# A two-layer decoder trunk on one core: 24 recurrent weight blocks are split inside the first MLP's block stream, the inverse's matrices are sent ahead of the operand copies, and the last chunk's output copies are reordered

## The chip, the cores and the metric

One core of a Trainium2 chip runs the whole kernel in one launch. The metric is the device time of that core in microseconds (us), lower is better. TensorE is called PE in the profile, VectorE DVE, ScalarE ACT, GpSimd POOL and SyncE SP; the last three also issue DMAs.

## The reference

512 tokens of width 1024 go through two layers in float32; each layer adds a mixer and then an MLP to the residual x, and one RMS norm ends the trunk.

```python
h = rms_norm(x, mixer_norm[0]); x = x + dsa_mixer(h, ...)       # indexer, top-k keys, attention
x = x + sqrelu_mlp(rms_norm(x, mlp_norm[0]), up[0], down[0])    # 1024 -> 4096 -> 1024
h = rms_norm(x, mixer_norm[1]); x = x + rwkv7_mixer(h, ...)     # recurrent layer
x = x + sqrelu_mlp(rms_norm(x, mlp_norm[1]), up[1], down[1])
return rms_norm(x, final_norm)

def sqrelu_mlp(h, w_up, w_down):
    u = jax.nn.relu(h @ w_up)
    return (u * u) @ w_down

# inside rwkv7_mixer, per head, over the 512 steps:
sa = einsum('bhvk,bhk->bhv', state, -kk_t)
state = state * w_t + sa[..., None] * b_t + v_t[..., None] * k_t
y = einsum('bhvk,bhk->bhv', state, r_t)
```

## The kernel before

**Weights.** All weight matrices lie in device memory as blocks of 128 x 1024 floats (512 KB), in one list `wblk`. A product in float32 quality is made from three products of a cheaper type: each operand is cut into a high and a low part (hi, lo), and `gemm` (L143 to L150) sends hi x hi, hi x lo and lo x hi, 24 matmuls of 512 columns for a block. `c.order` is the order in which blocks are used. `wdma` issues the next load on SP's queue: a raw pair of 1 MB where two blocks follow each other in the list, a single one otherwise. `wload` makes the parts: an ACT copy to hi (L122) and a DVE subtraction to lo (L130 through `sub`). `wget` hands out the next split block, with `prefetch` running two or so ahead in program order. Raw and split blocks live in the same ring of 21 buffers (`b8`, 8 KB per partition) as x, the activations and the larger tiles of the recurrent layer.

**Blocks split ahead of their layer.** The recurrent layer uses 39 blocks (numbers relative to `BASE`): 0 to 7 for the keys, 8 to 10 for the low-rank decay and gate inputs, 11 and 12 for the output gate, 13 to 20 for r, 21 to 28 for v, 29 and 30 for the gate's second factor, 31 to 38 for the output product. For the 36 in `PRE`, `presplit` does the splitting during the first MLP: in half blocks, 72 steps, each a load on POOL's queue (L78, 256 KB), the ACT copy (L86), the DVE subtraction (L87) and two stores to a scratch tensor `scr` on POOL's queue (L91, 256 KB each). `mlp` advances it by `SD` = 2 steps at each of the 16 output blocks of both up products and of the 8 of the first down product, until the 72 are done. The recurrent layer then loads hi and lo from `scr` (L98, 1 MB) with no splitting. Block 0 is in a raw pair with the MLP's last block and is split where it is used.

**First MLP.** Two halves; each has 16 up blocks, an activation (`act`, L300 to L304: DVE, two ACT squares, DVE) and 8 down products of two blocks each. The last three columns of the second half are done in two token halves, and `Keys.first` runs beside them.

**Start of the recurrent layer.** `rwkv` makes the key product over k = 0 to 7 with eight banks open (L811 to L813). For each k, `prep2` makes the mixed input and its parts (L757, L764, L766, L133, L130), and `others` makes those for the other products, among them `xr`, the input of the r product. Then follow two r blocks (`rgemm`), the key norms, the low-rank products and the gate product (L949 to L951).

**Inverse.** The chunks of 64 tokens need the inverse of a triangular 64 x 64 matrix for each head and chunk. `invert` is a generator advanced by `run`. Its first two steps send the diagonal 32 x 32 blocks of `Mt` to a scratch `dn` (L1042, two sets of 8 DMAs on SP's queue; the second needs the last `Mt`); the third loads them back as `tn` (L1047); then come 30 pairs of DVE operations that depend on each other (L1054, L1056), advanced by a budget `RUNW` at each of the 8 blocks of the v product; then copies and DMAs back into `Mt`. `run` is called once in the loop over m (`RQ`), once after `acopy(0)` and `c.prefetch(3)`, then with `RUNW`. `acopy` (L1181) copies operands `AR` to another place, 8 DMAs on SP's queue a chunk.

**Order.** Up to the v product the framework orders each engine's instructions by program position, shifted by the numbers in `PR` (a positive one puts a site earlier), and by what it takes to be ready. Every engine then executes its list in order, and so does each queue. From `while not stage` on, the order is that of the program.

**Chunks.** For each of 8 chunks: `step_z` (a product, then two ACT copies L1304), `step_u` (a product L1310, then four ACT copies L1314), the state update, `step_r` and `step_y`. `opn(n + 1, 1)` makes the second half of the next chunk's operands, with DVE masks (L1208). `out(0)` makes the first 256 tokens' input of the output product: eight steps of a DVE operation (L1413), an ACT copy to hi (L133) and a subtraction to lo on DVE or POOL. After the last chunk, `wom(0, m)` uses all eight.

Of the kernel before, what the change touches and what calls it, by code (L numbers as in the profile page):

```python
# [19 lines left out]
class Ctx:  # L20
# [51 lines left out]
    def presplit(s):  # L72
        nc = s.nc
        jobs = [(j, slice(h * 512, h * 512 + 512)) for j in s.scr for h in range(2)]

        def load(j, cs):
            raw = s.t("praw")
            nc.gpsimd.dma_start(raw, s.aps["wblk"][j][:, cs])  # L78
            return raw

        raws = [load(*v) for v in jobs[:2]]
        for i, (j, cs) in enumerate(jobs):
            r = raws.pop(0)
            hi, lo = s.t("phi", F32R), s.t("plo", F32R)
# [205 lines left out]
def mlp(c, x, mi, done, mid, side=iter(())):  # L290
# [15 lines left out]
    for half in range(2):  # L306
        s = Act(c, "s", 16)
        for m in range(16):
            for _ in range(SD):
                next(side, None)  # L310
            p = c.bank("g")
            c.gemm(p, c.wget(), a)
            wait.append((p, *s(m)))
            if rstd is None:
                if m == 0:
                    mi.n.stat()
                    continue
                rstd = mi.n.spread()
            while wait:
                act(*wait.pop(0))  # L320
        for m in range(KC - HM if half else KC):
            for _ in range(0 if half else SD):
                next(side, None)
# [475 lines left out]
def rwkv(c, x, ks, gi):  # L799
# [382 lines left out]

    acopy(0)
    c.prefetch(3)
    run(1)

    def opnd(n):
        if n > 1:
# [511 lines left out]
```

## Time and profile before

| | us |
|---|---|
| median of 3 runs (lowest, highest) | 1376.36 (1374.78, 1379.29) |
| the profiled execution's own time | 1375.36 |
| its span in the trace | 1373.6 |
| busy in the span: PE, DVE, ACT, POOL | 1294.9, 779.2, 602.1, 282.9 |

Starts are counted from the span's start. A row's bracket tells how long the engine was idle before it and what released it. PEclk is the granted TensorE clock: 1.00 is 2.4 GHz, 0.5 is 1.2 GHz. The DMA share is the mean busy share of the core's 16 DMA engines. PE's busy time counts pipelined matmuls and says little alone; how many matmuls fall in a stretch says more.

### The profile page before, as it was taken

How to read it: one execution, taken by the hardware profiler on the slowest of the kernel's cores; microseconds unless marked ns; L12 is line 12 of the kernel's file. 1: busy time of each engine (PE TensorE's matmuls, PEld its weight loads, DVE VectorE, ACT ScalarE, POOL GpSimd, SP SyncE). 2: the span in 40 equal slices, each digit the busy share in tenths (PEclk: the TensorE clock that was granted, in tenths of full speed). 3: DMA queues.
4: the chain of work that ended last, by engine and by line, in shares of the span. 5: the costliest groups of instructions: out<-in, count | busy, mean ns of one | idle time of the engine just before them, and what ended most of it. 6: DMA issues, size and time to landing. Idle time of an engine off the chain costs nothing.

```text
span 1373.6 us, 20666 instructions
## 1 busy us (share of the span) xinstructions
PE 1294.9 (94%) x8197; PEld 1060.9 (77%) x8197; DVE 779.2 (57%) x1382; ACT 602.1 (44%) x1053; POOL 282.9 (21%) x388
## 2 busy tenths in 40 slices
PE   7989899989899989999999996977999999999997
PEld 6767566877688867889867885767998888888887
DVE  5689984546544455523968877365755532245422
ACT  5545693445532344411866423766244421134421
POOL 0386751055443143000000001164200000000000
PEclk9999999999999999999999998998999999999998
DMA  7100014388988786542442383235222222322401
GB/s 287 62 31 31 1 42 150 112 311 305 300 308 267 263 289 234 173 164 70 192 153 93 87 297 79 49 85 208 101 102 83 92 92 94 121 92 83 163 1 62
DMA packets 80592, 196.78 MB, mean 143 GB/s; under 512 B 36336, under 2 KB 39024, under 8 KB 75248
## 3 DMA queue, kind: packets, MB, share of 16 engines
q1 hardware_dynamic: 60976, 136.59, 29.1%
q0 software_dynamic: 17280, 56.64, 11.9%
q10 hardware_dynamic: 2240, 2.24, 0.5%
q8 instruction: 64, 1.05, 0.3%
q14 instruction: 32, 0.26, 0.1%
HBM read 148.77 MB, written 44.56 MB: 141 GB/s over the span
## 4 chain that ended last, share of the span: by engine, by line
PE 65%; DVE 11%; DMA 11%; ACT 5%; issue 4%; POOL 3%; SPq 0%; ACTq 0%; DVEq 0%; POOLq 0%
PE g L148 15%; PE g L150 15%; PE g L149 15%; DMA praw<-in_wblk 9%; PE g L661 2%; POOL scr L91 1%; ACT phi L86 1%; DVE pr L1054 1%; DVE tn L1056 1%; PE d L646 1%; DVE rot L444 1%; DVE w L130 1%; ACT w L122 1%; DVE L L620 1%; PE g L1310 1%
## 5 line engine op out<-in xcount | busy, mean ns | idle before, releaser
L130 DVE TENSOR_TENSOR w<-wraw,w 128x1024 fp32r<-128x1024 f32 x150 | 183.0, 1243 | 98.1 <-ACT w L122 98.1
L148 PE MATMUL g<-ah,w 128*128 128x512 f32 x512 | 203.8, 398 | 15.8 <-ACT w L122 15.8
L150 PE MATMUL g<-sh,w 128*128 128x512 f32 (+1 forms) x608 | 216.3, 356 | 0.4 <-DVE w L130 0.4
L148 PE MATMUL g<-sh,w 128*128 128x512 f32 (+1 forms) x608 | 216.5, 356 | 0.0
L149 PE MATMUL g<-sl,w 128*128 128x512 f32 (+1 forms) x608 | 216.2, 356 | 0.0
L150 PE MATMUL g<-ah,w 128*128 128x512 f32 x512 | 202.9, 396 | 0.6 <-DVE w L130 0.5
L149 PE MATMUL g<-al,w 128*128 128x512 f32 x512 | 202.5, 395 | 0.0
L122 ACT ACTIVATE w<-wraw 128x1024 fp32r<-128x1024 f32 x155 | 157.9, 1047 | 99.9 <-DMA wraw<-in_wblk 85.0
L150 PEld LDWEIGHTS g<-sh,w 128*128 128x128 f32 x608 | 114.9, 189 | 17.0 <-DVE w L130 0.8
L149 PEld LDWEIGHTS g<-sl,w 128*128 128x128 f32 x608 | 114.9, 189 | 16.3
L148 PEld LDWEIGHTS g<-sh,w 128*128 128x128 f32 x608 | 114.9, 189 | 16.2
L148 PEld LDWEIGHTS g<-ah,w 128*128 128x128 f32 x512 | 98.2, 192 | 37.6 <-ACT w L122 17.5
L150 PEld LDWEIGHTS g<-ah,w 128*128 128x128 f32 x512 | 98.0, 191 | 24.1 <-DVE w L130 3.6
L302 ACT ACTIVATE sh<-r 128x512 fp32r<-128x512 f32 x64 | 40.4, 631 | 168.8 <-DVE r L300 168.8
L149 PEld LDWEIGHTS g<-al,w 128*128 128x128 f32 x512 | 98.3, 192 | 20.3
L87 DVE TENSOR_TENSOR plo<-praw,phi 128x512 fp32r<-128x512 f32 x72 | 49.1, 689 | 71.8 <-ACT phi L86 68.9
L304 DVE TENSOR_TENSOR sl<-q,sh 128x512 fp32r<-128x512 f32 x64 | 44.3, 693 | 65.8 <-ACT q L303 65.2
L86 ACT ACTIVATE phi<-praw 128x512 fp32r<-128x512 f32 x72 | 44.8, 626 | 81.2 <-DMA praw<-in_wblk 73.3
L300 DVE SCALAR_TENSOR_TENSOR r<-g,rstd 128x512 f32<-128x512 f32 x64 | 43.9, 688 | 56.5 <-PE g L150 50.6
L91 POOL DMA_DIRECT2D scr<-phi x72 | 38.9, 541 | 177.0 <-ACT phi L86 176.5
L208 ACT ACTIVATE sq<-x 128x256 f32<-128x256 f32 (+1 forms) x56 | 26.7, 499 | 105.5 <-DVE x L328 57.2
L328 DVE TENSOR_TENSOR x<-g,x 128x512 f32<-128x512 f32 x26 | 17.8, 689 | 77.6 <-PE g L150 77.6
(321 smaller groups left out, 2570.1 us busy)
## 6 DMA issues: line engine op xcount, KB each, us to landing
wraw<-in_wblk SPq DMA_DIRECT2D x77, 1024.0 KB, 4.9
w<-scr SPq DMA_DIRECT2D x35, 1024.0 KB, 6.4
praw<-in_wblk POOLq DMA_DIRECT2D x72, 256.0 KB, 5.2
scr<-phi POOLq DMA_DIRECT2D x72, 256.0 KB, 5.1
scr<-plo POOLq DMA_DIRECT2D x72, 256.0 KB, 5.9
wraw<-in_wblk SPq DMA_DIRECT2D x4, 512.0 KB, 4.7
x<-in_xT SPq DMA_DIRECT2D x8, 256.0 KB, 5.2
x<-in_xT SPq DMA_DIRECT2D x2, 1024.0 KB, 6.6
```

The lines of the kernel that those rows point to most:

```text
L86: nc.scalar.activation(hi, r, AF.Copy)
L87: nc.vector.tensor_sub(lo, r, hi.bitcast(F32))
L91: nc.gpsimd.dma_start(s.scr[j][:, e, cs], v.bitcast(F32))
L122: s.wsp = s.nc.scalar.activation(hi, r, AF.Copy)
L130: s.nc.vector.tensor_sub(out, a, b)
L148: s.nc.tensor.matmul(p, whi[:, kc, :], ahi, start=first and kc == 0, stop=False)
L149: s.nc.tensor.matmul(p, whi[:, kc, :], alo, start=False, stop=False)
L150: s.nc.tensor.matmul(p, wlo[:, kc, :], ahi, start=False, stop=last and kc == KC - 1)
L300: nc.vector.scalar_tensor_tensor(r, p, 0.0, rstd, op0=OP.max, op1=OP.mult)
L302: nc.scalar.activation(hi, r, AF.Square)
L304: nc.vector.tensor_sub(lo, q, hi.bitcast(F32))
L661: nc.tensor.matmul(po[HF[e]], v[sc // 2][:, j:j + 64], st8[tb, pr, e][:, sc], start=sc == 0, stop=sc == tb)
```

## The change

`presplit` is gone. `PRE` shrinks to the 24 blocks 15 to 38, which are put into `c.order` in pairs after every fourth block of the first three quarters of the first MLP. They are loaded raw on SP's queue in 1 MB pairs and split as whole blocks by `wload`; the new `keep`, called at every fourth output block of the up products and at every second of the first down product, takes two of them and stores hi and lo to `scr` on POOL's queue (512 KB each). `c.pos` tells the two places of a block in the order apart. The other 12 blocks (0 to 7 and 11 to 14) are loaded raw and split where the recurrent layer uses them. Two `run(1)` now stand ahead of `acopy(0)` and `c.prefetch(3)`; the priorities of `acopy` and `inv` and the budget `RUNW` change. In chunk 6, three steps of `out(0)` are put around `opn(7, 1)`; in chunk 7 no step stands ahead of `step_y`, `step_r` comes ahead of `step_u`, and five follow.

```diff
-    def presplit(s):
...
-            with s.hp("pre"):
-                nc.scalar.activation(hi, r, AF.Copy)
-                nc.vector.tensor_sub(lo, r, hi.bitcast(F32))
-                if i + 2 < len(jobs):
-                    raws.append(load(*jobs[i + 2]))
-                for e, v in enumerate((hi, lo)):
-                    nc.gpsimd.dma_start(s.scr[j][:, e, cs], v.bitcast(F32))
-            yield
+    def keep(s, n):
+        for _ in range(n):
+            i = s.wnext - len(s.ready)
+            if not s.pos[i]:
+                break
+            j = s.order[i]
+            for e, v in enumerate(s.wget()):
+                s.nc.gpsimd.dma_start(s.scr[j][:, e], v.rearrange("p a b -> p (a b)").bitcast(F32))
 
     def wdma(s):
-        if s.order[i] in s.scr:
+        if s.order[i] in s.scr and not s.pos[i]:
...
         for m in range(16):
-            for _ in range(SD):
-                next(side, None)
             p = c.bank("g")
             c.gemm(p, c.wget(), a)
+            if m % 4 == 3:
+                c.keep(keep)
...
+            if m % 2 and not half:
+                c.keep(keep)
...
-PR = {... 'acopy': 400, ... 'inv': -20, ...}
+PR = {... 'acopy': -50, ... 'inv': 50, ...}
...
+    run(1)
+    run(1)
     acopy(0)
     c.prefetch(3)
-    run(1)
...
+            if n == 6:
+                w0 = out(0)
+                pull(w0, 1)
             if n and more:
                 opn(n + 1, 1)
+            if n == 6:
+                pull(w0, 2)
...
-        w0 = out(0)
-        pull(w0, 4)
         n = NCH - 1
         step_z(n)
-        pull(w0, 2)
+        py = step_r(n)
         step_u(n)
-        pull(w0, 2)
-        c.prefetch(3)
-        py = step_r(n)
         step_y(n, py)
+        pull(w0, 5)
+        c.prefetch(4)
...
-RUNW = 3400
+RUNW = 3000
-PRE = (*range(8), 13, 14, 11, 12, *range(15, 39))
+PRE = tuple(range(15, 39))
...
+        od, pos, pre = list(range(26)), [0] * 26, [BASE + j for j in PRE]
+        for i in range(26, BASE):
+            od.append(i)
+            pos.append(0)
+            if i % 4 == 1:
+                pos += [1] * len(pre[:2])
+                od += pre[:2]
+                del pre[:2]
...
-        mlp(c, x, mi, lambda m, xm, h: n.add(xm, h), k.first(), c.presplit())
+        mlp(c, x, mi, lambda m, xm, h: n.add(xm, h), k.first(), 2)
```

## Rows read from the trace of the kernel before

**Rows 1.** The page's first part: busy time, share of the span, instructions.

```profile
PE 1294.9 (94%) x8197; PEld 1060.9 (77%) x8197; DVE 779.2 (57%) x1382; ACT 602.1 (44%) x1053; POOL 282.9 (21%) x388
```

**Rows 2.** Windows: PE, PEld, DVE, ACT, POOL busy (count), PEclk, DMA share, GB/s.

```profile
264.00:358.00 94.00, 88.78 (x388) 72.28 (x386) 53.30 (x76) 46.61 (x72) 43.42 (x82) 0.96 0.84 291
358.00:450.00 92.00, 87.29 (x371) 71.27 (x372) 40.01 (x49) 32.61 (x45) 36.85 (x69) 0.96 0.83 283
450.00:550.00 100.00, 93.11 (x394) 75.40 (x393) 54.57 (x71) 45.83 (x68) 34.21 (x64) 0.97 0.75 263
1030.00:1090.00 60.00, 60.00 (x267) 49.69 (x266) 29.84 (x35) 24.25 (x35) 0.00 (x0) 1.00 0.23 80
...
361.00:368.00 7.00, 5.68 (x13) 4.03 (x14) 4.95 (x6) 3.85 (x6) 3.23 (x6) 0.53 1.00 323
```

**Rows 3.** Waits from 264 to 600 us: engine, line, releaser, us, times, longest.

```profile
ACT phi L86 <- DMA praw<-in_wblk: 73.3, 33, 7.2
...
PE g L148 <- ACT w L122: 15.8, 4, 5.0
```

**Rows 4.** Timeline of ACT, then of PE, around 360 us.

```profile
355.40 1.35 ACT L86 ACTIVATE phi<-praw 128x512 fp32r<-128x512 f32 x2 [4.54 <-DMA praw<-in_wblk]
...
362.28 0.79 PE L148 MATMUL g<-ah,w 128*128 128x512 f32 x1 [4.45 <-ACT w L122]
```

**Rows 5.** Page, costliest groups: busy, mean ns of one, idle before.

```profile
L130 DVE TENSOR_TENSOR w<-wraw,w 128x1024 fp32r<-128x1024 f32 x150 | 183.0, 1243 | 98.1 <-ACT w L122 98.1
...
L122 ACT ACTIVATE w<-wraw 128x1024 fp32r<-128x1024 f32 x155 | 157.9, 1047 | 99.9 <-DMA wraw<-in_wblk 85.0
```

**Rows 6.** DMA issues, KB each, median us to landing: 270 to 530 us, then whole span.

```profile
wraw<-in_wblk SPq DMA_DIRECT2D x20, 1024.0 KB, 9.0
...
wraw<-in_wblk SPq DMA_DIRECT2D x77, 1024.0 KB, 4.9
```

**Rows 7.** Windows at the start of the recurrent layer, columns as in rows 2.

```profile
620.00:650.00 30.00, 30.00 (x254) 30.00 (x253) 10.20 (x28) 5.12 (x13) 0.00 (x0) 1.00 0.16 58
660.00:680.00 20.00, 20.00 (x104) 17.19 (x104) 20.00 (x33) 18.82 (x32) 0.00 (x0) 1.00 0.40 149
680.00:690.00 10.00, 10.00 (x46) 8.27 (x45) 5.21 (x8) 3.19 (x6) 0.00 (x0) 1.00 0.23 75
690.00:700.00 10.00, 10.00 (x42) 4.96 (x42) 4.70 (x6) 7.93 (x14) 0.00 (x0) 1.00 0.49 178
```

**Rows 8.** Timeline of SP's queue around the inverse.

```profile
764.22 3.64 SPq L1042 DMA_DIRECT2D dn<-Mt  x6
...
778.04 12.16 SPq L1181 DMA_DIRECT2D abd<-AR  x16
790.25 1.12 SPq L1042 DMA_DIRECT2D dn<-Mt  x2
...
792.80 6.37 SPq L1042 DMA_DIRECT2D dn<-Mt  x8
```

**Rows 9.** Timeline of DVE and PE around the inverse, and a window after it.

```profile
788.70 0.76 DVE L1028 TENSOR_TENSOR Mt<-g,kon 128x256 f32<-128x256 f32 x2
...
807.27 0.27 DVE L1054 TENSOR_TENSOR pr<-tn 128x60 f32<-128x60 f32 x1 [6.62 <-DMA tn<-dn]
...
842.43 0.22 DVE L1056 TENSOR_TENSOR tn<-tn,pr 128x60 f32<-128x60 f32 x1
...
846.96 0.44 PE L1213 MATMUL d<-AR,KB 64*64 64x128 f32 x1 [10.45 <-DVE BL L1208]
...
847.00:853.00 6.00, 6.00 (x50) 4.44 (x52) 2.71 (x7) 0.91 (x2) 2.65 (x3) 0.51 1.06 163
```

**Rows 10.** Timeline of ACT and PE at the last chunk.

```profile
947.80 0.42 ACT L133 ACTIVATE oh<-ot 128x256 fp32r<-128x256 f32 x1
...
951.97 1.21 ACT L1304 ACTIVATE bd<-g 64x512 f32<-64x512 f32 x2
...
953.23 1.12 PE L1310 MATMUL g<-bd,Mt 128*64 128x128 f32 x8 [5.79 <-ACT bd L1304]
```

More of the change, by code (lines that the diff above doesn't have):

```diff
@@ L70, in banks8 @@
         return out
-    def presplit(s):
[L73 to L84, printed above, removed]
-            with s.hp("pre"):
-                nc.scalar.activation(hi, r, AF.Copy)
-                nc.vector.tensor_sub(lo, r, hi.bitcast(F32))
-                if i + 2 < len(jobs):
-                    raws.append(load(*jobs[i + 2]))
-                for e, v in enumerate((hi, lo)):
-                    nc.gpsimd.dma_start(s.scr[j][:, e, cs], v.bitcast(F32))
-            yield
+    def keep(s, n):
[6 more added lines that the diff above has]
+                s.nc.gpsimd.dma_start(s.scr[j][:, e], v.rearrange("p a b -> p (a b)").bitcast(F32))
     def wdma(s):
         i = s.wend
-        if s.order[i] in s.scr:
+        if s.order[i] in s.scr and not s.pos[i]:
             w = s.b8("w", F32R, (128, 2, KC, 128))
@@ L287, in add, with mlp @@
         s.n.add(xk, h)
-def mlp(c, x, mi, done, mid, side=iter(())):
+def mlp(c, x, mi, done, mid, keep=0):
     nc = c.nc
@@ L321, in mlp @@
         for m in range(KC - HM if half else KC):
-            for _ in range(0 if half else SD):
-                next(side, None)
             p = c.bank("g")
@@ L374 @@
 TLS = False
-PR = {'a_stack': -1000, 'a_turn': 20, 'a_irope': 20, 'wsplita': 100, 'stata': 20, 'a_evac': -20, 'a_values': -20, 'vload': -100, 'turn': 3000, 'others': -20, 'mact': 100, 'gnorm': 200, 'acopy': 400, 'front': 3000, 'prep2': 50, 'out': -20, 'step_u': 400, 'rhat': 50, 'inv': -20, 'bonus': 100, 'wsplitm': -1000, 'back': 100, 'rg0': -100, 'step_r': -1000, 'rnorm': 50, 'middle': 3000, 'g2': -100, 'norm': 20, 'vmean': -100, 'statc': 200, 'opt': -20, 'pre': -500}
+PR = {'a_stack': -1000, 'a_turn': 20, 'a_irope': 20, 'wsplita': 100, 'stata': 20, 'a_evac': -20, 'a_values': -20, 'vload': -100, 'turn': 3000, 'others': -20, 'mact': 100, 'gnorm': 200, 'acopy': -50, 'front': 3000, 'prep2': 50, 'out': -20, 'step_u': 400, 'rhat': 50, 'inv': 50, 'bonus': 100, 'wsplitm': -1000, 'back': 100, 'rg0': -100, 'step_r': -1000, 'rnorm': 50, 'middle': 3000, 'g2': -100, 'norm': 20, 'vmean': -100, 'statc': 200, 'opt': -20, 'pre': -500}
 TB = 4
@@ L1572 @@
 ORDER = list(range(8)) + list(range(13, 13 + RA)) + list(range(8, 13)) + list(range(13 + RA, 39))
-SD = 2
-PRE = (*range(8), 13, 14, 11, 12, *range(15, 39))
+PRE = tuple(range(15, 39))
 GP = ()
@@ L1657, in build @@
         c.single = (*SG, BASE + 8)
-        c.order[BASE:] = [BASE + j for j in ORDER] + list(range(BASE + max(ORDER) + 1, len(c.order)))
+        od, pos, pre = list(range(26)), [0] * 26, [BASE + j for j in PRE]
[6 more added lines that the diff above has]
+                del pre[:2]
+        c.order = od + [BASE + j for j in ORDER] + list(range(BASE + max(ORDER) + 1, len(c.order)))
+        c.pos = pos + [0] * (len(c.order) - len(pos) + 1)
         c.open(ctx)
```

## The prediction

> **What bounds the kernel now.** I read the page first: PE is busy for 94% of the span, DVE for 57%, ACT for 44% [rows 1]. PE is the bound, so a change can only pay where PE stands still or runs at half clock, and the question is where that is. The windows answer it. In the second MLP 267 matmuls fall in 60 us, 0.2247 us each, at clock 1.00; in the three windows of the first MLP's first three quarters 388, 371 and 394 matmuls fall in 94, 92 and 100 us [rows 2]. At full pace 1153 matmuls take 259 us, and the windows are 286 us: **27 us are lost there**. The waits give the reason: PE waits four times for the hi part of a weight block, 15.8 us in all, and in the same stretch ACT stands 73.3 us, 33 times, on half blocks that `presplit` loads [rows 3]. The timeline shows one case: ACT stands 4.54 us on such a load, behind it stands the hi copy of the block that PE needs, and PE stands 4.45 us [rows 4]. The other 11 us are the clock: in the 7 us from 361 us on it is 0.53 and 13 matmuls run where 31 would fit [rows 2]. Apart from this stretch two single waits of PE lie where the change works, one behind the inverse and one in the last chunk; they come below.
>
> **First MLP: removed and added.** Removed are 72 half-block steps; added are 24 whole-block splits. What starves PE is the load on the DMA engines. Four blocks keep PE busy for 4 x 24 x 0.2247 = 21.6 us. Before, an up product wants in that time 2 MB of weights and 8 steps of 0.25 MB in and 0.5 MB out, 8 MB in all (MB of 1024 KB), 388 GB/s; a down product wants 5 MB, 243 GB/s. The windows show 263 to 291 GB/s at a DMA share of 0.75 to 0.84 [rows 2], so the up product asks for more than it gets and the steps fall behind. After, every four blocks come with two kept ones: 3 MB in, 2 MB out, 5 MB, 243 GB/s throughout. The row nearest to that is the window of the down product, 358 to 450 us: its 8.6 us of loss are the wait of 4.45 us [rows 4], which began before it in the up product, and the half clock behind it; the rest of it ran at full pace although the backlog kept the DMA share at 0.83 [rows 2].
>
> Does the new stream fit in its buffers? Of 21 there go 2 to x, 4 to the normed input and 8 to the activation, so 7 are left: one in use by PE, two with the kept pair until its stores land, one raw pair, three split blocks ahead, which last 3 x 5.4 = 16 us. A load landed in 9.0 us in the crowded stretch, in 4.9 us over the span [rows 6], and hi and lo take 1.05 and 1.24 us [rows 5]: 11.3 us at worst, under 16. The kept blocks pass without waiting for PE, and POOL's queue holds nothing but their stores. So the four waits should go. ACT still stands in line for raw loads, though, so I leave 3 us and take **a gain of 24 us**; the ends are 27 (all) and 13.5 (half).
>
> **Start of the recurrent layer: added.** Twelve blocks are no longer ready in `scr`; block 0 was split here already, so 11 splits are added, 11.5 us of ACT and 13.7 us of DVE [rows 5]. The blocks needed before 655 us find DVE and ACT mostly idle: from 620 to 650 us they are busy for 10.2 and 5.1 of 30 us [rows 7]. The costly ones are blocks 4 to 7, 13 and 14, whose buffers come free late: from 660 to 680 us DVE is busy for all 20 us and ACT for 18.8 [rows 7], and six splits there are 7.5 us of DVE ahead of `others`. What is late next is `xr`, which the first r product needs part by part; DVE's idle time, 4.8 us from 680 and 5.3 us from 690 us [rows 7], covers it only from about 686 us on. PE runs full there (46 matmuls in the 10 us from 680), so what is not covered is PE's loss. With two splits done early, four remain, 5 us, less some 2.5 us of lead of PE's order over `xr`. I take **a loss of 2.5 us**, and 1 us for blocks 11 and 12 ahead of the gate product, together 3.5; the ends are 0 and 8. The loads get smaller here (0.5 MB raw for 1 MB from `scr`), which I cost at nothing.
>
> **Inverse: moved.** SP's queue first sends six of the first eight blocks at 764 us, then takes 16 operand copies from 778 on (12.16 us, most of it waiting for `AR`), and the second set of eight leaves at 792.80, one every 0.80 us [rows 8]. The last `Mt` was written by 789.4 [rows 9]. With the copies behind, the second set can leave 3.4 us earlier and at the 0.61 us a piece of the first set [rows 8], 1.5 us more: 4.9 us. The 30 pairs start on DVE when `tn` lands, 807.27, and end at 842.6; PE resumes 4.4 us later, when the masks behind them are done [rows 9]. This chain ends last there, so 4.9 us carry through. Moved past on the queue are 8 or 16 operand copies, first used at `step_z`, and the load of the third v block, needed two blocks, 11 us, after the last `Mt`; if it falls behind the two `tn` loads it costs up to 2 us. The budget of 3000 for 3400 starts one block earlier and changes nothing in the sum. I take **a gain of 5 us**; the ends are 0 and 13 (10.45 us of wait and half of the 6 us at clock 0.51 [rows 9]).
>
> **Last chunk: moved.** Four ACT copies of `out`, one every 1.04 us from 947.80, stand ahead of `step_z`'s copies at 951.97, and `step_u` waits for these until 953.23 [rows 10]. After, three steps are still ahead of them in ACT's order, one of them before DVE's masks, which it delays by about as much. So the copies start 1 to 2 us earlier, not 4, and `step_r` fills a part of the rest. Against that, five steps now stand behind `step_y`, 5.2 us, beside a first output product of some 2.9 us. I take **a gain of 1 us**; the ends are a gain of 5 and a loss of 2.3.
>
> **The sum.** 24 - 3.5 + 5 + 1 = 26.5 us off the profiled execution's 1375.36 us is 1348.9. The median of the runs is 1.0 us above that execution, so I predict 1350. All good ends together give 45 us, 1331; all bad ones a gain of 3, 1373.
>
> **Rivals.**
> *Half of the waits stay.* ACT is in order, and a raw pair that is late still stands ahead of the square copies and of the next hi copy. For it: ACT's waits in [rows 4] are of that kind. Against it: 243 GB/s wanted for 388. It gives 10.5 us less, 1360.
> *DVE becomes the bound at the start of the recurrent layer.* All 11 splits on the path, 13.7 us, and one stretch of half clock, some 4 us, in place of 3.5: 1364. For it: 20 busy us in 20 [rows 7]. Against it: the idle time before and behind.
> *The inverse does not start earlier.* The v loads go out ahead of it as soon as buffers are free, and its small transfers land behind them: the change does not do what it says, 1355.
> *Slower: kept blocks starve the stream.* The kept pair is loaded on SP's queue ahead of the next blocks that PE needs. If less than 11.3 us of split blocks are ahead, two blocks or fewer, each of the 12 pairs costs one load, 4.9 us [rows 6]: 59 us, 1409. That fewer than three are ahead is the point from which it decides; against it stand the 7 free buffers. The Trainium skill (DMA: Bandwidth & Descriptors, section Queues, rings and completion order) says that each DMA engine takes turns between the queues that have work; by it, a kept load that leaves POOL's queue for SP's no longer shares the engines with the stream but stands in its line, which speaks for this rival. The trace shows only that the stream's loads slowed beside POOL's queue; it cannot tell turns from bytes.
>
> **How the numbers follow.** Forecast 0.62; half of the waits 0.12; DVE the bound 0.10; inverse not earlier 0.08; slower 0.08. Leaving out the last and the tails of the bounds, the range is 1336 to 1368. A difference of 0.3% (4.1 us) is about what can be told from none for this kernel. Faster by more: 0.87; within: 0.05; slower: 0.08.
>
> **What would show it.** Right: in the first MLP's three quarters PE has no wait of over 2 us on a hi copy, its clock stays 1.00, DMA goes at some 240 GB/s, and about 60 / 267 us a matmul hold from end to end. The first L1054 starts about 5 us earlier relative to the last `Mt`, and PE's wait before the second set of masks is 5 to 6 us. `step_u` of chunk 7 still waits for ACT, 3 to 4 us. From 655 to 700 us DVE has six more L130 and PE a wait of some 2 us ahead of the r product. Wrong: waits of PE on L122 in the first MLP behind kept blocks, or SP's queue standing on a buffer that a kept block's store holds.

## The result, and the profile after

| | before | after |
|---|---|---|
| median of 4 runs each on one chip, us | 1377.82 (1374.78 to 1380.98) | 1362.01 (1360.74 to 1363.17) |
| ratio of after to before, 95% interval | | 0.9885 (0.9858 to 0.9911) |
| the profiled execution's own time, its span | 1375.36, 1373.6 | 1363.17, 1361.0 |

The changed kernel is faster by 1.15%, some 16 us by the medians and 12.2 by the two profiled executions. Forecast were 1350 us and 26.5 us of gain. Five points of the program, read from both traces, say in which stretch the gain came and went:

| point | before, us | after, us | gain so far |
|---|---|---|---|
| start of the key product's last matmul | 692.71 | 671.49 | 21.2 |
| last `Mt` written | 789.45 | 774.93 | 14.5 |
| first product of `step_z`, chunk 0 | 852.58 | 835.64 | 16.9 |
| end of the output product | 1008.64 | 996.21 | 12.4 |
| last matmul | 1367.19 | 1354.51 | 12.7 |

So the first MLP gave 21.2 us, the start of the recurrent layer took 6.7 of them, the inverse gave 2.4, and the chunks took 4.5. All line numbers of the changed kernel are 12 or 13 lower: the hi copy of a weight block is L109 (before L122), its lo part L117 (L130), the products L135 to L137, the masks L1196.

**First MLP.** The page's first part, then windows of the changed kernel (PE, PEld, DVE, ACT, POOL busy with counts, PEclk, DMA share, GB/s); they answer to [rows 1] and [rows 2].

```profile
PE 1294.1 (95%) x8197; PEld 1060.0 (78%) x8197; DVE 778.1 (57%) x1345; ACT 593.5 (44%) x1016; POOL 191.8 (14%) x220
```

```profile
264.00:358.00 94.00, 91.05 (x400) 74.73 (x399) 49.10 (x60) 41.08 (x58) 8.67 (x16) 0.96 0.54 194
358.00:450.00 92.00, 92.00 (x408) 76.17 (x407) 39.17 (x38) 28.46 (x29) 8.47 (x16) 1.00 0.77 272
450.00:550.00 100.00, 100.00 (x443) 82.81 (x442) 56.12 (x61) 47.08 (x64) 8.46 (x16) 1.00 0.65 233
292.00:299.00 7.00, 6.21 (x14) 4.43 (x15) 3.97 (x4) 2.59 (x3) 0.00 (x0) 0.52 0.77 279
```

From 358 us on PE runs at full pace: 408 matmuls where 371 ran before, 443 where 394 did. The first window still lacks some 28 of the 428 that fall in it where nothing waits (`old_split_even`, below): one wait, and 7 us at half clock behind it. The waits from 264 to 600 us (engine, line, releaser, us, times, longest) answer to [rows 3]; four waits of PE have become one, though ACT still stands 62.7 us on raw loads.

```profile
ACT w L109 <- DMA wraw<-in_wblk: 62.7, 14, 11.7
...
PE g L135 <- ACT w L109: 2.9, 1, 2.9
```

The timeline of ACT around that wait, then PE's; it lies at the first kept pair.

```profile
286.22 1.99 ACT L109 ACTIVATE w<-wraw 128x1024 fp32r<-128x1024 f32 x2
290.60 0.63 ACT L289 ACTIVATE sh<-r 128x512 fp32r<-128x512 f32 x1 [2.39 <-DVE r L287]
291.13 0.61 ACT L290 ACTIVATE q<-r 128x512 f32<-128x512 f32 x1
291.65 2.94 ACT L109 ACTIVATE w<-wraw 128x1024 fp32r<-128x1024 f32 x3
```

```profile
289.45 0.39 PE L137 MATMUL g<-ah,w 128*128 128x512 f32 x1
292.75 0.80 PE L135 MATMUL g<-ah,w 128*128 128x512 f32 x1 [2.91 <-ACT w L109]
```

ACT was not waiting for a load here: by the landing times in the trace, the block of that hi copy had been in its buffer since 267.53, 24 us before ACT came to it. ACT stood idle for 2.39 us ahead of `sh`, the square of the relu of the product that PE was just finishing, and the hi copy that PE needed next stood *behind* `sh` in ACT's list. So PE's wait is the way from the end of one product through DVE's relu, two squares and the first hi copy: 3.30 us from matmul to matmul.

**Start of the recurrent layer.** The timeline of DVE behind the key norms, and a window later on.

```profile
679.85 3.35 DVE L880 RECIPROCAL ry<-ru 128x512 f32<-128x512 f32 x1 [0.70 <-ACT ru L879]
...
684.57 1.22 DVE L117 TENSOR_TENSOR w<-wraw,w 128x1024 fp32r<-128x1024 f32 x1
685.71 0.68 DVE L883 SCALAR_TENSOR_TENSOR ro<-ru,ry 128x512 f32<-128x512 f32 x1
686.31 1.22 DVE L117 TENSOR_TENSOR w<-wraw,w 128x1024 fp32r<-128x1024 f32 x1
687.56 1.38 DVE L887 TENSOR_TENSOR rt<-ro,rt 32x512 fp32r<-32x512 f32 x2
```

```profile
763.00:767.00 4.00, 4.00 (x12) 3.16 (x11) 4.00 (x9) 0.00 (x0) 0.00 (x0) 0.57 0.01 4
```

Blocks 11 and 12 are split between the last steps of the key norms, 2.4 us of DVE ahead of `rt` and of all that follows. The sums of squares take 5.92 us instead of 4.21 and start 0.6 us later, since ACT comes late to the squares. That is 4.7 us, and the gate product indeed starts 25.74 us behind the start of the key product's last matmul, 4.9 later than before. The other 1.8 us come later, at the half clock from 763 us on (12 matmuls in 4 us); `split_only` below, which runs that stretch at 1.00, loses 5.0 us in this stage and not 6.7.

**Inverse.** SP's queue, DVE's first and last pair and the two waits of PE; they answer to [rows 8] and [rows 9].

```profile
774.62 4.67 SPq L1029 DMA_DIRECT2D dn<-Mt  x6
779.94 0.34 SPq L1034 DMA_DIRECT2D tn<-dn  x1
780.33 0.95 SPq L1029 DMA_DIRECT2D dn<-Mt  x2
...
784.66 0.34 SPq L1034 DMA_DIRECT2D tn<-dn  x1
```

```profile
789.85 0.27 DVE L1041 TENSOR_TENSOR pr<-tn 128x60 f32<-128x60 f32 x1 [1.21 <-DMA abd<-AR]
```

```profile
826.01 0.22 DVE L1043 TENSOR_TENSOR tn<-tn,pr 128x60 f32<-128x60 f32 x1
```

```profile
784.36 0.33 PE L1213 MATMUL d<-ident,KB 128*128 128x128 f32 x1 [2.18 <-DVE BL L1196]
```

```profile
830.49 0.44 PE L1201 MATMUL d<-AR,KB 64*64 64x128 f32 x1 [5.17 <-DVE BL L1196]
```

The second set leaves by 781.28, 6.35 us behind the last `Mt`, where it was 9.7. The chain starts 14.9 us behind the last `Mt`, where it was 17.8. (The view names an operand copy as what released it, but the pair reads `tn`, and the second `tn` load landed at 789.82, just ahead of it.) The chain itself takes 36.4 us for 35.4: four pieces of the v product's input (L753, L117) stand between its pairs on DVE, where there were three. From its end to `step_z` it takes 9.4 us for 9.9. So 2.9 - 1.0 + 0.5 are the 2.4 us of this stage. PE's wait falls from 10.45 to 5.17 us. New is a wait of 2.18 us inside the v product, for masks that DVE makes later there; it does not lengthen the stage, since PE still stands 5.17 us behind it for the chain.

**Last chunk.** ACT, PE and POOL around it; they answer to [rows 10].

```profile
934.28 0.81 ACT L120 ACTIVATE oh<-ot 128x256 fp32r<-128x256 f32 x2 [2.96 <-DVE ot L1401]
...
936.42 1.21 ACT L1292 ACTIVATE bd<-g 64x512 f32<-64x512 f32 x2
...
943.18 0.60 ACT L1345 ACTIVATE y<-g 128x512 f32<-128x512 f32 x1 [1.85 <-PE g L1340]
943.68 0.71 ACT L120 ACTIVATE oh<-ot 128x256 fp32r<-128x256 f32 x2
945.61 0.81 ACT L120 ACTIVATE oh<-ot 128x256 fp32r<-128x256 f32 x2 [1.22 <-DVE ot L1401]
947.54 0.42 ACT L120 ACTIVATE oh<-ot 128x256 fp32r<-128x256 f32 x1 [1.12 <-DVE ot L1401]
```

```profile
932.80 1.07 PE L1290 MATMUL g<-sv,abd 128*64 128x64 f32 x15 [1.26 <-DVE abd L1196]
...
937.67 0.69 PE L1298 MATMUL g<-bd,Mt 128*64 128x128 f32 x4 [2.88 <-ACT bd L1292]
```

```profile
948.04 0.73 POOL L115 TENSOR_TENSOR ol<-ot,oh 128x256 fp32r<-128x256 f32 x1 [1.21 <-ACT oh L120]
```

The wait ahead of `step_u` is down from 5.79 to 2.88 us, but the first output product starts 13.0 us behind the start of the last `step_z`, where it was 12.9. The wait was filled and moved, not won: `step_z` (from 930.85 us on) now stands 1.26 us in its middle on DVE's masks, `step_r` fills another 1.1 us, and `step_z`'s copies (L1292) begin 5.57 us behind its start, where they began 5.79, because ACT stood 2.96 us on DVE for two steps of `out` that are still ahead of them. `step_u` starts 0.2 us earlier. And now five of the eight operand copies of the output product stand behind `step_y`'s evacuation, so that its first block takes 5.3 us (943.84 to 949.16, the start of the second) instead of 3.0.

### The profile page after: what moved, and what is told of

Read it like the earlier page. It is cut to its first block, busy times and chain, and to the rows that moved or that the text cites. A ratio compares the mean times of both kernels' runs of the same rounds, so it can differ in the third digit from the quotient of the medians.

```text
span 1361.0 us, 20178 instructions
## 1 busy us (share of the span) xinstructions
PE 1294.1 (95%) x8197; PEld 1060.0 (78%) x8197; DVE 778.1 (57%) x1345; ACT 593.5 (44%) x1016; POOL 191.8 (14%) x220
## 4 chain that ended last, share of the span: by engine, by line
PE 79%; DVE 12%; ACT 4%; issue 2%; DMA 2%; POOL 1%; SPq 1%; DVEq 0%; ACTq 0%; POOLq 0%
PE g L137 20%; PE g L135 20%; PE g L136 20%; PE g L648 2%; DVE rot L431 1%; DVE tn L1043 1%; DVE pr L1041 1%; PE d L633 1%; DVE acc L517 1%; DVE L L607 1%; DVE m L515 1%; PE g L1298 1%; PE g L1013 1%; ACT bd L1292 1%; PE d L406 1%
## 5 line engine op out<-in xcount | busy, mean ns | idle before, releaser
L117 DVE TENSOR_TENSOR w<-wraw,w 128x1024 fp32r<-128x1024 f32 x185 | 224.2, 1239 | 125.9 <-ACT w L109 125.9
L109 ACT ACTIVATE w<-wraw 128x1024 fp32r<-128x1024 f32 x190 | 193.0, 1048 | 141.4 <-DMA wraw<-in_wblk 119.1
L135 PE MATMUL g<-sh,w 128*128 128x512 f32 (+1 forms) x608 | 216.5, 356 | 0.0
L137 PE MATMUL g<-sh,w 128*128 128x512 f32 (+1 forms) x608 | 216.1, 355 | 0.0
L135 PE MATMUL g<-ah,w 128*128 128x512 f32 x512 | 201.0, 393 | 2.9 <-ACT w L109 2.9
L137 PE MATMUL g<-ah,w 128*128 128x512 f32 x512 | 200.3, 391 | 0.0
L135 PEld LDWEIGHTS g<-sh,w 128*128 128x128 f32 x608 | 114.9, 189 | 16.2
L137 PEld LDWEIGHTS g<-sh,w 128*128 128x128 f32 x608 | 114.9, 189 | 16.2
L135 PEld LDWEIGHTS g<-ah,w 128*128 128x128 f32 x512 | 96.8, 189 | 23.1 <-ACT w L109 3.3
L137 PEld LDWEIGHTS g<-ah,w 128*128 128x128 f32 x512 | 96.8, 189 | 21.0 <-DVE w L117 0.8
L79 POOL DMA_DIRECT2D scr<-w x48 | 25.6, 536 | 295.9 <-ACT w L109 285.8
L617 ACT ACTIVATE L<-L,st 128x256 f32<-128x256 f32 (+3 forms) x64 | 35.1, 552 | 15.1 <-DVE st L615 15.1
L290 ACT ACTIVATE q<-r 128x512 f32<-128x512 f32 x64 | 39.4, 615 | 0.0
```

What stands on the lines that cost most here:

```text
L109: s.wsp = s.nc.scalar.activation(hi, r, AF.Copy)
L117: s.nc.vector.tensor_sub(out, a, b)
L135: s.nc.tensor.matmul(p, whi[:, kc, :], ahi, start=first and kc == 0, stop=False)
L137: s.nc.tensor.matmul(p, wlo[:, kc, :], ahi, start=False, stop=last and kc == KC - 1)
L290: nc.scalar.activation(q, r, AF.Square)
L617: nc.scalar.activation(L[g][:, :n], L[g][:, :n], AF.Exp, bias=nmx[:, g:g + 1], scale=0.125, accum_out=sm[:, g:g + 1])
```

## The experiments

Each kernel ran beside the kernel before on the same chip (its medians there lay from 1376.27 to 1378.80 us). Stage times below are differences of the same points as in the table above.

### Which part gives what

`split_only` is the change without the edits on the inverse and on the last chunk; `no_inverse` and `no_lastchunk` each undo one of these two.

```diff
# no_inverse
-    run(1)
-    run(1)
     acopy(0)
     c.prefetch(3)
+    run(1)
-RUNW = 3000
+RUNW = 3400
# (and acopy 400, inv -20 as before)
```

```diff
# no_lastchunk
+        w0 = out(0)
+        pull(w0, 4)
         step_z(n)
-        py = step_r(n)
+        pull(w0, 2)
         step_u(n)
+        pull(w0, 2)
+        c.prefetch(3)
+        py = step_r(n)
         step_y(n, py)
-        pull(w0, 5)
-        c.prefetch(4)
# (and the three pulls behind step_y of chunk 6 are gone)
```

> The first part of the change alone: 24 blocks split in the stream, 11 more split in the recurrent layer, the rest as before. Theory A (from the traces): 21 us gained in the first MLP, 6.7 us lost between the end of the key product and the last matrix of the inverse; 14.5 us below the kernel before, 1363 us, with the window from 264 to 550 us almost free of waits. Theory B (the prediction's terms): 24 and 3.5, 20.5 us below, 1357 us.

> The changed kernel with the inverse's part undone: the operand copies and the prefetch stand ahead of the second and third step of the inverse again, with the old priorities and the old budget. Theory A (read from the two traces): the part gained some 5 us at PE's wait behind the inverse and gave 3 us back inside the v product, where PE now stands 2.6 us on masks; so undone it costs 2 us net, 1364 us, with PE's wait back at 10 us and the 2.6 us wait in the v product gone. Theory B (the prediction): the 5 us carry through, 1367 us. Theory C: the wait in the v product comes from the splitting ahead of it and stays; then 1367 us with both waits.

> The changed kernel with the last chunk's part undone: all eight steps of the output's input stand behind chunk 6 and ahead of step_y again. Theory A (from the traces): the part leaves the wait of step_u as long as it was in sum and makes the first output product wait for its last steps, 5.4 us in place of 2.9; undone it gains 2.7 us, 1359.3 us. Theory B (the prediction): the part gains 1 us, so undone 1363 us.

| | median, us | ratio to before | key product to last `Mt` | last `Mt` to `step_z` | `step_z` to the output product's end |
|---|---|---|---|---|---|
| before | 1377.82 | 1 | 96.7 | 63.1 | 156.1 |
| after | 1362.01 | 0.9885 | 103.4 | 60.7 | 160.6 |
| `split_only` | 1359.08 | 0.9881 (0.9849 to 0.9913) | 101.7 | 62.8 | 157.0 |
| `no_inverse` | 1363.77 | 0.9909 (0.9881 to 0.9937) | 103.3 | 63.7 | 160.5 |
| `no_lastchunk` | 1357.64 | 0.9865 (0.9839 to 0.9891) | 103.4 | 60.1 | 157.7 |

The splits alone are worth as much as the whole change. The edit on the inverse gives 3.0 us in its stage (63.7 to 60.7); without it PE's wait is back and the v product has none:

```profile
832.18 0.44 PE L1200 MATMUL d<-AR,KB 64*64 64x128 f32 x1 [11.91 <-DVE BL L1195]
```

The edit on the last chunk costs 2.9 us in its stage (160.6 against 157.7). All kernels of this document bear it out: from the first output matmul to the end of the output product the five that have this last chunk take 52.4 us each, the eight with the old one 49.6. Undone, the larger wait comes back, and the time is shorter all the same:

```profile
935.14 1.12 PE L1298 MATMUL g<-bd,Mt 128*64 128x128 f32 x8 [5.78 <-ACT bd L1292]
```

### What made the old kernel wait in the first MLP

Two theories: the bytes that the crowded half asked for, or the old form of code, with half blocks on a queue of their own. `old_split_thin` is the kernel before with 20 blocks for 36, one half-block step where there were two; `old_split_even` is the kernel before with all 36 blocks, the 72 steps spread over all four products.

```diff
# old_split_thin
-SD = 2
-PRE = (*range(8), 13, 14, 11, 12, *range(15, 39))
+SD = 1
+PRE = tuple(range(19, 39))
```

```diff
# old_split_even
-            for _ in range(SD):
+            for _ in range(SD + (m % 4 == 3)):
-            for _ in range(0 if half else SD):
+            for _ in range(2 * SD + m % 2):
-SD = 2
+SD = 1
```

> The kernel before with its old half-block splitting at a lower rate: one step at each output block in place of two, for the 20 blocks 19 to 38, the others split where they are used. The DMA demand beside the up products falls from 388 to 243 GB/s; the form (half blocks, loads and stores on POOL's queue, ACT waiting in order) stays. Theory A (demand): of the 27 us that PE loses in the first MLP before, at most 5 stay. Theory B (form: ACT stands on half-block loads and the next block's hi copy behind it): half or more stays, 14 us or more, and PE waits of 4 to 5 us on the hi copy are still there.

> The kernel before with its old half-block form of splitting, but all 36 recurrent blocks split evenly over the whole first MLP (72 steps over its four products, by the bytes about 280 GB/s instead of 388 in its crowded half and 243 in the thin one). Theory A (bytes per time made the waits, and inline splits cost the recurrent layer's start 5 us or more): the first MLP has at most a few us of waits, the key product's end to the last Mt takes 97 us as in the kernel before, and the time is 1346 to 1352 us. Theory B (the old form waits as soon as more than 24 blocks go through it, or early in the first half where the ring is not yet filled): 5 to 15 us of waits in the first MLP, 1358 to 1368 us.

`old_split_thin` took 1353.08 us in its one run, `old_split_even` 1348.75 (1345.70 to 1349.94), a ratio of 0.9784 (0.9755 to 0.9814). Neither has a wait in the first MLP; the key product ends 27.2 and 26.0 us earlier than before, all of the 27 us that [rows 2] showed lost. The windows of `old_split_even`:

```profile
264.00:358.00 94.00, 94.00 (x428) 78.24 (x427) 57.17 (x77) 49.09 (x76) 32.06 (x60) 1.00 0.74 243
358.00:450.00 92.00, 91.97 (x406) 75.78 (x406) 39.41 (x48) 28.73 (x38) 33.68 (x63) 1.00 0.85 300
450.00:550.00 100.00, 100.00 (x443) 82.81 (x442) 61.12 (x77) 52.71 (x79) 36.51 (x69) 1.00 0.82 268
```

It moves 300 GB/s from 358 to 450 us without a loss, more than the 283 of [rows 2] in a window that lost. So the mean rate isn't what starved PE, nor is the old form by itself; what is left is the crowding into half the products. How crowding became a wait stands in ACT's timeline of the kernel before, around its first wait (PE stands from 305.2 to 310.6 us):

```profile
300.73 0.63 ACT L86 ACTIVATE phi<-praw 128x512 fp32r<-128x512 f32 x1 [3.97 <-DMA praw<-in_wblk]
302.73 0.63 ACT L302 ACTIVATE sh<-r 128x512 fp32r<-128x512 f32 x1 [1.36 <-DVE r L300]
303.26 0.61 ACT L303 ACTIVATE q<-r 128x512 f32<-128x512 f32 x1
305.25 1.35 ACT L86 ACTIVATE phi<-praw 128x512 fp32r<-128x512 f32 x2 [1.37 <-DMA praw<-in_wblk]
307.95 0.63 ACT L302 ACTIVATE sh<-r 128x512 fp32r<-128x512 f32 x1 [1.36 <-DVE r L300]
308.49 0.61 ACT L303 ACTIVATE q<-r 128x512 f32<-128x512 f32 x1
309.01 0.61 ACT L86 ACTIVATE phi<-praw 128x512 fp32r<-128x512 f32 x1
309.53 1.04 ACT L122 ACTIVATE w<-wraw 128x1024 fp32r<-128x1024 f32 x1
```

Two half blocks came late, each held up ACT and, through its lo part on DVE, the relu; the hi copy that PE needed stood behind both, at 309.53. Its own block had landed at 269.56; in all four waits the whole block had been there for 17 to 40 us. Spread out, fewer late half blocks stand ahead of a hi copy. How much of that is the load's lateness and how much the number of copies in line, these two runs don't separate.

### What waits in the new stream

First by demand: `kept_bunched` takes four kept blocks for two at each point of the first half, `kept_late` leaves out the first kept pair and takes four blocks at the last.

```diff
# kept_bunched
-                pos += [1] * len(pre[:2])
+                pos += [1] * len(pre[:4])
-        mlp(..., k.first(), 2)
+        mlp(..., k.first(), 4)
# kept_late
-            if i % 4 == 1:
+            if i % 4 == 1 and i > 29:
+                m = 4 if i == 73 else 2
# (m for the 2 of the three lines below it, and 4 for 2 in the call of mlp)
```

> The changed kernel with the kept blocks bunched: in the first half of the first MLP's stream four of four blocks are kept pairs until the 24 are done where the change spread them, so that while they run the stream asks the DMA engines for about as much as the old kernel's crowded half did (388 GB/s by the prediction's count), and the second half has none. Theory A (the demand for bytes made the waits): waits of 2 to 5 us on the split copies return between 264 and about 420 us, in sum 10 us or more, and the first MLP ends 10 us or more later than in the changed kernel; about 1372 us. Theory B (the old waits came from the form of the old code, half blocks whose stores and loads lay in the way): the block stream stays free of waits, and the time is that of the change, 1360 to 1364 us.

> The changed kernel with the first kept pair left out of its place (the pair comes at a later point, four blocks instead of two). Theory A (the one wait of 3.30 us at 289 us and the half clock behind it come from the first kept pair meeting a ring that is not yet filled ahead): the wait goes, no half clock at 292, the key product ends 5 to 6 us earlier, 1356 to 1358 us. Theory B (any first kept pair makes this wait, wherever it comes): the wait turns up at the next kept pair with the same 3 us, and the time stays at 1361 to 1364 us.

`kept_bunched`: 1392.30 us in one run; the key product ends 30.9 us later than in the changed kernel. `kept_late`: 1363.14 us in one run; no wait at the place of the first pair but a gap of 1.40 us at 311.74, and one of 4.52 us at 529.78, where four blocks stand together. The first lost more than the theory of demand says (10 us), the second met neither of its theories: its key product ends 1.3 us later than the changed kernel's. The places of the waits speak against demand as the main cause. In `kept_bunched` PE is late in the up products behind 290.77 us (by 5.19), 320.97 (3.30), 348.35 (3.30) and 375.71 (4.72), once for each kept point there, the fourth just behind the last of them. At the first three the block that PE needed had landed 23.2, 10.8 and 7.7 us before ACT copied it. At the fourth the load was late on top of that: ACT came to it and stood another 1.31 us.

```profile
379.33 2.01 ACT L109 ACTIVATE w<-wraw 128x1024 fp32r<-128x1024 f32 x2 [1.31 <-DMA wraw<-in_wblk]
```

In the down products, where no `sh` stands ahead, PE is late by 5.27 us behind 404.03 on a load (landed at 408.11, copied at 408.19) and by 1.85 behind 434.21. So where the kept blocks are bunched, loads come late too; but most of the waits in the up products are there without that. `kept_late`'s wait of 4.52 us is again one of 3.30 and a load that came 1.1 us after ACT did.

So I counted, in ACT's order of the first 16 up products, the hi copies that stand ahead of each `sh`, less those of all blocks of the stream, kept ones too, up to that of the next product. Below zero the next product's hi copy stands behind the `sh` that waits for the product before it:

| kernel | lead at `sh` of products 0 to 15 | PE waits at product |
|---|---|---|
| after | 2, 1, 0, **-1**, 1, 1, 2, 1, 1, 1, 2, 1, 1, 1, 2, 1 | 3 |
| `kept_bunched` | 2, 1, 0, **-3**, 1, 1, 2, **-1**, 1, 1, 2, **-1**, 1, 1, 2, **-1** | 3, 7, 11, 15 |
| before, `old_split_even` | never below 0 | (late half blocks; none) |

`wget` splits two blocks ahead of the one in use. A kept block in the list is one of these two, so behind a kept pair no product's block is ahead by this rule alone. The framework's order can still put a hi copy earlier, and did so at all points of the changed kernel but the first; why not there stays open. Counted over all 32 up products, the lead falls below zero once more in `kept_late` (the last product) and twice more in `pre_28` below (products 11 and 15 of the second half), and in the kernels with kept blocks these, and those of the table and of `stream_single28` below, are all the places where PE is late by 3.30 us or more behind an up product. At -3, in `kept_bunched`, two more hi copies of 0.95 us stand ahead of the one that PE needs: 3.30 + 1.89 = 5.19 us.

The Trainium skill (Perfetto Trace Analysis, section Tensor Engine Instruction (MATMUL, LD_WEIGHTS)) says that ScalarE and VectorE take their instructions strictly in order, while TensorE may pull weight loads ahead. The trace agrees: ACT's 2.39 idle us at 290.60 are put down to the relu, and the three hi copies follow at 291.65 with no wait of their own.

Two more kernels test order against transfers. `stream_single28` (with the last chunk of before) keeps 28 blocks one at a time, after every second block and on into the last down product, so that the demand is spread as thinly as it can be; `stream_ahead3` differs from it in the lookahead alone, three blocks for two.

```diff
# stream_single28
-PRE = tuple(range(15, 39))
+PRE = tuple(range(11, 39))
-            if i % 4 == 1:
-                pos += [1] * len(pre[:2])
+            if i % 2 and i > 27:
+                pos += [1] * len(pre[:1])
-            if m % 4 == 3:
+            if m % 2:
                 c.keep(keep)
-            if m % 2 and not half:
-                c.keep(keep)
+            c.keep(keep)
# (and 1 for 2 in the call of mlp, and the last chunk of before)
```

```diff
# stream_ahead3, against stream_single28
-            for e, v in enumerate(s.wget()):
+            for e, v in enumerate(s.wget(3)):
-            c.gemm(p, c.wget(), a)
+            c.gemm(p, c.wget(3 if keep else 2), a)
# (and so for the two products of a down block)
```

> The changed kernel with its last chunk undone, with 28 kept blocks instead of 24, and with the kept blocks put into the stream one at a time (after every second block, and on into the last down product) instead of in pairs. Theory A (what the stream still loses in the first MLP comes from kept blocks in lumps, and the front's loss from blocks 11 to 14 split inline): no wait over 1.5 us in the first MLP, key product to last Mt 97 us, so 1357.6 less 5.5 less 6.7 us, about 1345 to 1347 us. Theory B (a kept block costs the stream a wait wherever it stands): waits of 1 to 3 us at several of the 28 points, 1352 us or more.

> The kernel with 28 kept blocks one at a time (1382.0 us, seven waits of 3.30 us in the first MLP at 200 GB/s), changed in one thing: the first MLP's block stream is asked to run three blocks ahead of the one in use instead of two, so that the hi copy of the next product's block stands ahead of the relu's copies on ScalarE's queue. The bytes and the transfers are the same. Theory A (the waits come from the order on ScalarE: kept blocks use up the two blocks of lookahead, so the next block's hi copy stands behind a copy that itself waits for the product before): the seven waits go, the clock stays at 1.00, the key product ends 33 to 37 us earlier, key product to last Mt 97 us: 1345 to 1349 us. Theory B (the waits come from the transfers, kept blocks holding buffers of the ring or the stores crowding the loads): one more block ahead takes one buffer more, the waits stay or grow: 1375 us or more.

`stream_single28`: 1382.00 us (1379.02 to 1384.32), ratio 1.0036 (1.0014 to 1.0057), slower than the kernel before. My Theory A of that expectation (lumps) fell: seven waits of 3.30 us, three of them in the first 16 products at 301.43, 328.49 and 355.56 us. The count, with leads of 2, 1, 1, 0, 1, **-1**, 1, 1, 1, **-1**, 1, 1, 1, **-1**, 1, 1, puts them at products 5, 9 and 13, and there they are; in the second half it puts four at 1, 5, 9 and 13, and there are the other four. An eighth late start, of 1.85 us behind 289.22 on a lo part, is not in the count. ACT's timeline at the third:

```profile
356.71 0.63 ACT L289 ACTIVATE sh<-r 128x512 fp32r<-128x512 f32 x1 [4.22 <-DVE r L287]
357.24 0.61 ACT L290 ACTIVATE q<-r 128x512 f32<-128x512 f32 x1
357.76 2.94 ACT L109 ACTIVATE w<-wraw 128x1024 fp32r<-128x1024 f32 x3
```

The block of that first hi copy had landed at 343.52. `stream_ahead3`: 1345.24 us (1343.94 to 1347.98), ratio 0.9762 (0.9740 to 0.9784). All eight are gone, and the key product ends 39.4 us earlier. Windows of `stream_single28`, then of `stream_ahead3`:

```profile
264.00:550.00 286.00, 265.97 (x1129) 215.46 (x1128) 125.05 (x140) 100.51 (x129) 23.67 (x44) 0.96 0.59 202
```

```profile
264.00:550.00 286.00, 286.00 (x1275) 237.31 (x1274) 143.34 (x159) 118.58 (x151) 27.84 (x52) 1.00 0.69 240
```

The same blocks, the same bytes, one block more ahead: 1129 matmuls become 1275, and the rate rises from 202 to 240 GB/s because PE asks for more. A longer lookahead would help against late loads as well, so this pair alone does not tell the two apart. The landing times do: at the seven waits of `stream_single28` the block that PE needed had landed 14.2 to 28.7 us before ACT copied it. Transfers were not its bound.

### The start of the recurrent layer

`pre_28` is the changed kernel with blocks 11 to 14 kept as well, four at each of the last two kept points of the first MLP.

```diff
-PRE = tuple(range(15, 39))
+PRE = tuple(range(11, 39))
-                pos += [1] * len(pre[:2])
+                m = 4 if i > 65 else 2
+                pos += [1] * len(pre[:m])
# (m in the two lines below it too, and 4 for 2 in the call of mlp)
```

> The changed kernel with 28 instead of 24 kept blocks (four at the last two points of the first MLP), so that the last blocks which the change splits beside the key product and the norms are split earlier. Theory A (the front's loss of 6.7 us between the key product's end and the last Mt comes from the inline splits on VectorE and ScalarE ahead of the norms): the loss falls to 2 to 4 us, about 1358 to 1360 us. Theory B (the loss is the half clock and the order of the masks, not the splits): the loss stays at 6 to 7 us and the time at 1361 to 1364 us.

1369.06 us in one run: the wait at the first pair is still there, and the points with four blocks add two (3.30 us at 513.35, 4.54 at 541.60). But from the key product to the last `Mt` it takes 96.6 us, as the kernel before does (96.7), and `stream_ahead3` with the same 28 blocks takes 96.6 too. So all of the front's loss comes from these four of the eleven inline splits; the other seven, blocks 1 to 7, cost nothing in this stage. The half clock at 763 us went with it; why it was there stays open.

### Toward a better kernel

`even_inv` adds the change's edit on the inverse to `old_split_even`. `even_inv_mid` adds to that the change's last chunk with the five late copies put ahead of `step_y`.

```diff
# even_inv_mid, last chunk, against after
         py = step_r(n)
+        pull(w0, 3)
         step_u(n)
+        pull(w0, 2)
         step_y(n, py)
-        pull(w0, 5)
```

> The kernel with the old half-block splits of all 36 blocks spread evenly over the first MLP (1348.8 us, last Mt to the first state product 63.5 us), and now the change's part on the inverse (matrices and priorities) added; the last chunk stays as in the kernel before. Theory A (the part on the inverse is worth 2.5 to 3 us by itself, as the stage times of the changed kernel with and without it say): last Mt to the first state product 60 to 61 us, the wait of 10 us behind the v product down to about 5 us, in all 1345.5 to 1346.5 us. Theory B (it helps only where the recurrent layer's front is late): the stage stays at 63 us, 1348 to 1349 us.

> even_inv with the last chunk as the change has it, but for one thing: the last five operand copies are put ahead of the chunk's step_u and step_y (three behind step_r, two behind step_u) and not behind step_y. Theory A (the change's last chunk loses because five copies stand on ScalarE and VectorE behind step_y's evacuation): the first output block takes 2.9 us instead of 5.4, the wait ahead of step_u stays at about 3 us instead of 6, so the stage from the last step_z to the second output block is 2 to 4 us shorter than in the kernel before: 1342 to 1344 us. Theory B (whatever stands between costs as much elsewhere, the copies then delay the evacuation that step_u or step_y waits for): within 1 us of even_inv.

`even_inv`: 1343.43 us (1341.40 to 1344.80), ratio 0.9734 (0.9714 to 0.9754), the lowest median of all, though its interval overlaps that of `stream_ahead3`. From the last `Mt` to `step_z` it takes 61.2 us for 63.5, a gain of 2.3; the other 3 us by which its median lies under `old_split_even`'s I don't credit to the edit: in the two profiled executions 3.1 us are there when the first MLP's products begin (219.63 for 222.74 us), and up to there the two don't differ in code. `even_inv_mid`: 1346.39 us (1343.02 to 1350.34), ratio 0.9758 (0.9732 to 0.9784); Theory A fell, and by the medians, 3.0 us apart, so did Theory B. Its first output block takes 3.1 us, as hoped, and the wait ahead of `step_u` is 2.88 us. But from `step_z` to the output product's end it takes 157.9 us against 156.6. Of these 1.3 us, 0.9 lie between the last `step_z` and the first output product, 13.1 us for 12.1; the kernels with the old last chunk lie there between 12.1 and 13.1 too, so no loss is shown, but no gain either. ACT's timeline suggests why:

```profile
929.64 1.58 ACT L1315 ACTIVATE sv<-g 64x256 f32<-64x256 f32 x4
931.25 0.42 ACT L133 ACTIVATE oh<-ot 128x256 fp32r<-128x256 f32 x1
932.55 0.42 ACT L133 ACTIVATE oh<-ot 128x256 fp32r<-128x256 f32 x1 [0.89 <-DVE ot L1414]
933.06 0.60 ACT L1358 ACTIVATE y<-g 128x512 f32<-128x512 f32 x1
```

From `step_u`'s copies to `y` ACT goes without a stop but for DVE; moving copies about in this chain does not shorten it. That this chain sets the end is read from these rows, not tested by itself.

## Why the prediction was right in sign and too high in size

The time came at 1362, inside the range of 1336 to 1368, with 12.2 us of gain in the profiled executions for a forecast of 26.5. By its terms:

- **First MLP: 24 us forecast, 21.2 measured.** Right in size. The mechanism was half right: spreading out the work on the recurrent blocks does take the old waits away, as both old-form kernels show, in full. The step that failed is the counting of demand, 388 against 243 GB/s, as what decides: 300 GB/s ran without loss in `old_split_even`, 202 with seven waits in `stream_single28`. What decides is what stands ahead of the hi copy on ACT. The 3 us left for "ACT still stands in line for raw loads" were nearly the right sum for another cause, which is luck: one wait of 3.30 us and the half clock behind it, on `sh`, with the load long landed.
- **"Three split blocks ahead, which last 16 us".** This step failed. Buffers were free, but the program asks for two blocks ahead and counts kept ones among them. The slower rival named its condition, two blocks ahead or fewer, and it decided at one of twelve kept points; the price was not a load of 4.9 us but 3.30 us and the clock, and the cause was ACT's order, not a load. With singles the rival came true in its condition and its sign: `stream_single28` is slower than before.
- **Start of the recurrent layer: a loss of 3.5 forecast, 6.7 measured**, inside the ends of 0 and 8. The place was wrong. `xr` and blocks 4 to 7 cost nothing; the 1 us given to blocks 11 and 12 was 2.4, since they stand between the norm's last steps on DVE, and 2.3 came through ACT's squares. Both went when blocks 11 to 14 were kept; that the first share belongs to 11 and 12 is read from DVE's rows, not tested apart. The rest, 1.8, came with the clock.
- **Inverse: 5 forecast, 2.4 measured** (3.0 against `no_inverse`, 2.3 in `even_inv`). The 3.4 us of earlier start came (9.7 to 6.35). The 1.5 us from a quicker spacing did not: the first six pieces of the second set took 4.67 us, 0.78 each as before, and 0.5 us went in landing. That left 2.9 us. The step that failed after it is "the budget of 3000 for 3400 starts one block earlier and changes nothing in the sum": with one more piece of the v product's input between its pairs the chain takes 1.0 us longer, in every kernel that has this edit (36.4 to 36.5 us for 35.4).
- **Last chunk: a gain of 1 forecast, a loss of 2.9 measured**, past the bad end of 2.3. The cost was priced about rightly, five copies beside a product of 2.9 us: the output product took 2.8 us longer. The gain that was set against it failed at the step "the copies start 1 to 2 us earlier": `step_z`'s copies began 0.2 us earlier behind its start, since ACT still stood on DVE for the steps of `out` ahead of them. The 2.91 us by which PE's wait fell went mostly into a new wait on the masks and into `step_r`.

Of what would show it: full pace at 1.00 held from 358 us on, PE's wait in the inverse is 5.17 (5 to 6 said), that ahead of `step_u` 2.88 (3 to 4 said); no wait ahead of the r product, where 2 us were said. The four measured stages, 21.2 - 6.7 + 2.4 - 4.5, make the 12.4 us by which the output product ends earlier; of the 4.5, 2.8 lie in the output product, the edit's cost, and 1.6 between the first `step_z` and the last one, ahead of the last chunk's `step_z` (95.2 us for 93.6). That stretch takes 93.6 to 95.3 us in all kernels here, with either last chunk; what moves it stays open.

Two rivals named times near the result, 1360 and 1364, but not what happened: not half of the old waits stayed but none, and DVE did not become the bound for all 11 splits, only for two of them.

## What to carry to other kernels

Where an engine executes its list in order, ask of each thing that PE needs next what stands ahead of it in that list, and what that waits for; a lookahead counted in items shrinks as soon as other items are put into the same stream, and one item more of it was worth 37 us here. To tell order from a late transfer, compare when a block landed with when it was copied: here the waits of exactly 3.30 us had their block 7.7 to 28.7 us early, and those of 4.52 to 4.72 us had a late load on top. And a wait that an edit shortens is a gain only if what comes behind it starts earlier: measure from one step's start to a later one's, not the wait.

## What was not expected of the hardware

PE's granted clock fell to half at 763 us in the changed kernel (0.57 over 4 us) with no gap between matmul starts of over 0.45 us from 725 us on, and why stays open; `split_only`, with nearly the same work there, ran that stretch at 1.00. In the first MLP one wait of 3.30 us was followed by 7 us at 0.52: of the 28 matmuls that the window to 358 us lacks, 6.3 us, the wait itself is 3.1, and the clock took as much again.
